# Loading the first row of a row-sum kernel by four strided loads of 32 partitions instead of one of 128

## Chip, cores, metric

One core of one Trainium2 chip. The metric is device time in microseconds (us) of one execution. The kernel before takes 162.29 us (median of 6 runs, 162.17 to 162.41).

## The reference

```python
def setup_inputs():
    batch, seq, dim = 32, 512, 1024
    return {"x": np.random.randn(batch, seq, dim).astype(np.float32)}

def reference(x):
    return np.sum(x, axis=-1).astype(np.float32)
```

16384 rows of 1024 floats are summed; 67.11 MB are read, next to nothing is written.

## The kernel before

The rows are laid over 128 partitions, 112 of them per partition in the first block and 16 in the second. VectorE sums tiles of 16 rows per partition; three tile buffers rotate. ScalarE helps at the very end only. Of the first tile, the first row of each partition has a load of its own. Two loads (`EARLY`) are moved ahead of the barrier with which the program opens.

```python
EARLY = 2
...
        while c < whole:
            m = min(G, whole - c)                       # G = 16 rows
            xt = xpool.tile([P, G * D], F32, tag="xt", name="xt")
            parts = (0, 1, m) if done + c == 0 else (0, m)
            for i, k in zip(parts, parts[1:]):
                nc.sync.dma_start(
                    out=xt[:, i * D : k * D], in_=x_b[:, (c + i) * D : (c + k) * D]
                )
            a = ACT_ROWS if done + c + m == full else 0
            rows_dve(xt, res, 0, m - a, c)
...
# after compiling: the first EARLY loads are taken out of the body and put before the opening barrier
    loads = [i for i in code if i.engine == sp][:EARLY]
...
    code[at:at] = loads
```

## Time and profile before

| | before |
|---|---|
| time | 162.29 us |
| span in the profile | 160.6 us |
| DMA engines occupied by the load queue | 97.2% |
| VectorE busy | 121.5 us (76%) |
| first reduce starts | 22.00 us |

The kernel is bound by its stream of loads: the 16 DMA engines go from one packet to the next without a gap, and everything else fits beside them. The prediction shows the lines for this.

### The profile page before, as it was taken

The page shows a single profiled execution, that of the slowest core. Times are in us where ns is not written, and L with a number is a line of the kernel's source. Part 1 is how long each engine was busy: PE and PEld are TensorE (multiplying, and loading weights), DVE is VectorE, ACT ScalarE, POOL GpSimd, SP SyncE. Part 2 cuts the span into 40 slices and gives each one's busy share as a digit, 9 for nine tenths or more (in the row PEclk, how much of TensorE's full clock was granted, in tenths as well). Part 3 has the DMA queues.
Part 4 walks back from the last instruction along what each step waited for, and adds up shares of the span by engine and source line. Part 5 has one row for each costly group of instructions (what it writes and reads, how often), then busy time and mean ns, then how long its engine had stood idle before and what let it go on. Part 6 is the DMA issues. An engine that isn't in the chain of part 4 may idle for free.

```text
span 160.6 us, 119 instructions
## 1 busy us (share of the span) xinstructions
DVE 121.5 (76%) x16; ACT 17.2 (11%) x31; POOL 0.2 (0%) x4
## 2 busy tenths in 40 slices
DVE  0000059997799959999499994999949998697884
ACT  0000000000000000000000000000000000695892
POOL 0000000000000000000000000000000000000000
DMA  9988996996996996996996996996996996998991
GB/s 375 490 367 367 490 522 277 506 522 277 506 522 261 522 522 261 522 522 261 522 506 277 522 506 277 522 506 277 522 506 277 522 490 294 441 431 364 436 390 44
DMA packets 2160, 67.18 MB, mean 418 GB/s; under 512 B 496, under 2 KB 624, under 8 KB 880
## 3 DMA queue, kind: packets, MB, share of 16 engines
q1 hardware_dynamic: 2016, 67.12, 97.2%
q10 hardware_dynamic: 144, 0.06, 0.1%
HBM read 67.11 MB, written 0.07 MB: 418 GB/s over the span
## 4 chain that ended last, share of the span: by engine, by line
DMA 75%; DVE 23%; SPq 0%; issue 0%; DVEq 0%
DMA xt<-in_x_dram 75%; DVE res L43 21%; DVE pairs L59 1%; SPq L95 0%; DVE seen L112 0%; DVE part L59 0%; DVE res L59 0%; DVEq L120 0%
## 5 line engine op out<-in xcount | busy, mean ns | idle before, releaser
L43 DVE TENSOR_REDUCE res<-xt 128x16 f32<-128x16384 f32 (+3 forms) x9 | 119.8, 13309 | 36.5 <-DMA xt<-in_x_dram 36.5
L51 ACT ACT_TABLE_LOAD x1 | 1.3, 1283 | 138.1 <-DMA xt<-in_x_dram 138.1
L51 ACT ACTIVATE xt<-xt 128x1024 f32<-128x1024 f32 x15 | 15.6, 1044 | 2.4 <-DMA xt<-in_x_dram 2.3
L51 ACT ACTIVATION_READ_ACCUMULATOR xt<-xt 128x1 f32 x15 | 2.8, 187 | 0.0
L59 DVE CUSTOM_DVE_ANT_0 pairs<-xt 128x512 f32<-128x512 f32 (+1 forms) x2 | 1.1, 567 | 0.2 <-DMA xt<-in_x_dram 0.2
L59 DVE CUSTOM_DVE_ANT_0 pairs<-xt,part 128x240 f32<-128x240 f32 x1 | 0.5, 468 | 0.0
L112 DVE COPY seen<-part 128x1 f32<-128x1 f32 x1 | 0.2, 153 | 0.0
L59 DVE DVE_READ_ACCUMULATOR2_ANT res<- 128x1 f32 x2 | 0.2, 83 | 0.0
L157 POOL MEMSET const-uint8-127<- 128x1 uint8 x1 | 0.1, 102 | 0.0
L157 POOL MEMSET const-bfloat16-1.0<- 128x1 bf16 x1 | 0.1, 101 | 0.0
L157 POOL MEMSET const-float32-0.0<- 128x1 f32 x1 | 0.1, 99 | 0.2 <-issue 0.2
L157 POOL MEMSET const-float32-1.0<- 128x1 f32 x1 | 0.1, 99 | 0.0
L59 DVE DVE_READ_ACCUMULATOR2_ANT part<- 128x1 f32 x1 | 0.1, 83 | 0.0
## 6 DMA issues: line engine op xcount, KB each, us to landing
xt<-in_x_dram SPq DMA_DIRECT2D x1, 7680.0 KB, 21.5
xt<-in_x_dram SPq DMA_DIRECT2D x1, 4608.0 KB, 32.5
xt<-in_x_dram SPq DMA_DIRECT2D x1, 2048.0 KB, 37.1
xt<-in_x_dram SPq DMA_DIRECT2D x1, 1024.0 KB, 39.1
xt<-in_x_dram SPq DMA_DIRECT2D x1, 512.0 KB, 3.8
xt<-in_x_dram SPq DMA_DIRECT2D x1, 272.0 KB, 39.3
xt<-in_x_dram SPq DMA_DIRECT2D x1, 240.0 KB, 39.4
xt<-in_x_dram SPq DMA_DIRECT2D x6, 40.8
```

Source lines behind the costliest of these rows:

```text
L43: nc.vector.tensor_reduce(out=res[:, c : c + n], in_=xt[:, j * D : (j + n) * D].rearrange("p (j d) -> p j d", d=D), axis=X, op=ADD,)
L51: nc.scalar.activation(out=v, in_=v, func=COPY, accum_out=acc)
L59: nc.vector.tensor_tensor_reduce(out=pairs[:, 0 : h - a], in0=xt[:, a:h], in1=xt[:, h:b], scale=1.0, scalar=first, op0=ADD, op1=ADD, accum ...
L112: nc.vector.tensor_copy(out=seen, in_=part)
L157: nc = _bacc.Bacc("TRN2", target_bir_lowering=False, num_devices=1)
```

## The change

The intent: shorter loads, of 128 KB in place of 512, were to get all engines going sooner, and every fourth partition was taken in place of blocks of 32.

```diff
-EARLY = 2
+EARLY = 5
...
-            parts = (0, 1, m) if done + c == 0 else (0, m)
-            for i, k in zip(parts, parts[1:]):
+            parts = [(slice(None), 0, m)]
+            if done + c == 0:
+                parts = [(slice(q, P, 4), 0, 1) for q in range(4)] + [(slice(None), 1, m)]
+            for q, i, k in parts:
                 nc.sync.dma_start(
-                    out=xt[:, i * D : k * D], in_=x_b[:, (c + i) * D : (c + k) * D]
+                    out=xt[q, i * D : k * D], in_=x_b[q, (c + i) * D : (c + k) * D]
                 )
```

## The prediction

What named a mechanism that no trace or run of this case shows is cut, and the cuts are marked: a paragraph of background, the reason given for a smaller spread, a reason for rival 1, and the mechanism of rival 2. The sum: 3.43 - 0.27 + 0.03 = 3.19 us, of whose gain of 0.24 I took 0.15, so 162.1. The 0.27 was my estimate, from the measured spread of 0.356 us taken in proportion to the rows of a load, 0.356 x 32 / 128 = 0.09; no run shows that the spread goes with the rows. The 0.03 is counted: in the profile the load queue has 16 packets of 4 bytes and 9 ns for each load, and its packets rose from 2016 to 2064 with three more loads. The 0.32 us of rival 2 is an estimate as well, twice the measured 0.159 us of a packet, and rival 3's reason is a supposition.

> **What bounds the kernel now.** I began with the page's busy shares and its DMA lines, to see which resource is full.
>
> ```profile
> DVE 121.5 (76%) x16; ACT 17.2 (11%) x31; POOL 0.2 (0%) x4
> ...
> DMA  9988996996996996996996996996996996998991
> ...
> q1 hardware_dynamic: 2016, 67.12, 97.2%
> ```
>
> VectorE is busy for 76% of the span, but the load queue occupies all 16 DMA engines for 97.2% of it. The sixes in the row of DMA tenths are no gaps: a 64 KB packet takes about 2.42 us and is counted in one slice, so slices of 4 us hold now one and now two of them per engine. Read from the records of single packets, each engine goes from one 64 KB packet to the next with nothing between. 8.39 MB (16 rows of 128 partitions) pass every 19.34 us, which is 434 GB/s.
>
> Next the chain of work that ended last, in order of time (start, length, what), to see whether VectorE ever holds the DMA back.
>
> ```profile
> 1.19 0.07 issue
> 1.26 39.99 DMA xt<-in_x_dram
> ...
> 41.27 17.23 DVE res L43
> ...
> 58.52 40.78 DMA xt<-in_x_dram
> ...
> 117.43 39.13 DMA xt<-in_x_dram
> 156.55 0.02 issue
> 156.58 0.69 DVE pairs L59
> ```
>
> The chain steps through VectorE because the load that it then follows was issued when a reduce freed its buffer. That must not be read as VectorE holding the end: the load issued at 58.52 landed 40.78 us later although its own packets need only 19.34. It stood in line for the other half. The packet records say the same: the load issued at 39.24 has its first packet at 59.50, so the line is never empty. A reduce takes 17.22 us and a load 19.34, so VectorE has 2.1 us to spare in every stage. The 1.7 us of VectorE at the end of the chain start when the last pieces land, and move with them.
>
> So the time is: when the DMA stream starts, plus a stream at a fixed rate, plus a fixed tail. The part that the change touches is the start. The same kernel by stretches of time (stretch, length, VectorE, ScalarE, GpSimd, clock, DMA share, GB/s):
>
> ```profile
> 0.00:1.00 1.00, 0.00 (x0) 0.00 (x0) 0.20 (x4) 1.00 0.00 0
> 1.00:2.00 1.00, 0.00 (x0) 0.00 (x0) 0.00 (x0) 1.00 0.94 164
> 2.00:3.00 1.00, 0.00 (x0) 0.00 (x0) 0.00 (x0) 1.00 2.12 897
> ```
>
> And the DMA issues, with the us from issue to landing:
>
> ```profile
> xt<-in_x_dram SPq DMA_DIRECT2D x1, 7680.0 KB, 21.5
> ...
> xt<-in_x_dram SPq DMA_DIRECT2D x1, 512.0 KB, 3.8
> ```
>
> Nothing moves in the first microsecond, and in the second 164 GB/s, well under half of 434, although the engines count as 94% busy: the packets are slow, not absent. (The 897 of the next line is the 60 KB packets credited as they start.) The records give the detail. The first load is issued from 0.000 to 0.376 and the second from 0.426 to 0.850. The first packets start on the 16 engines between 1.000 and 1.356. An engine carries eight 4 KB packets of the first row; most take 0.159 us, but 28 of the 128, mostly the first two of an engine, take 0.20 to 0.83, and the eight take 1.82 us on average (29.13 us over 16 engines) where 8 x 0.159 = 1.27 would do. The engines then start on the second load between 2.705 and 3.431, mean 3.00. This spread does not heal: before the last 64 KB packets, engines stand between 134.454 and 135.144, again 0.69 apart. A load has landed only when the slowest engine is through, so **the start of the slowest engine on the second load, 3.43 us, is what the change has to lower.**
>
> [...]
>
> **The change part by part.** It removes one issue of 512 KB and adds four of 128 KB (32 packets of 4 KB each). Bytes, packet size and number of packets stay the same; the three additional loads bring 3 x 16 semaphore packets, of 9 ns each, about 0.03 us per engine. All later loads keep their order. Five loads now stand before the opening barrier instead of two, and the other engines' waits on the first tile name five landings instead of two.
>
> Issue: the first load's 0.376 and a gap of 0.050 make 0.43 us per issue; the five loads at the end of the kernel, issued back to back at 116.569 to 118.412, are 0.46 apart. I assume that a load of 32 rows costs the same, as an issue seems mostly fixed. The second load then goes out at 4 x 0.43 = 1.7 us (1.84 at 0.46) instead of 0.43. From issue to first packet it took 1.000 in the first load and 0.845 in the final store (158.356 to 159.201), so its packets are ready on the first engine at 2.55 to 2.84, and 0.36 later on the last, if the spread of 1.000 to 1.356 is repeated: 2.9 to 3.2. That is close to the 2.705 to 3.431 at which the engines came to it before. The later issue costs nothing on the slow engines and holds the quick ones a little.
>
> Start:[...] The last engine then starts near 1.09, up to 0.27 earlier. The work after that is the same eight packets, the cold ones included, for they appear on every engine until about 2.0 us whatever its start. Each quarter brings an engine two packets, 0.32 us when warm, for 0.43 us of issue; but cold packets fill the difference for the first two quarters, so that only the quick engines run dry.
>
> Sum for the slowest engine: 3.43 - 0.27 (start) + 0.03 (semaphores) = 3.19, against a gate of 2.9 to 3.2 from the issue. I take half to two thirds of the 0.24 that this leaves, because the cold packets are a matter of chance, one unlucky engine sets the end, and the gate is so near: 0.15 us. 162.24 - 0.15 = 162.1.
>
> Beside other work, at no cost: the barrier opens near 2.5 us instead of 1.19, but VectorE first works at 22.0, and the next load, issued at 1.26 until now, is not reached in the line before 20.8. The three further waits of some 20 ns on VectorE and SyncE fall into its 2.1 us of slack.
>
> **The rivals.** (1) *The issue becomes the gate.* One issue of a load took 0.617 us (the fourth of the kernel). Were each quarter to cost that plus 0.05, the second load would go out at 2.67 and reach the last engine near 2.67 + 1.36 = 4.0: +0.6, so 162.8.[...] Against: 0.376 and 0.328 are the commoner values. (2)[...] a warm packet may take up to 0.32 us; six of them add 0.95 at worst, 163.2.[...] (3) *Cold packets shrink.* If they came from 128 rows being asked for at once, asking for 32 would make them quick: row done at 1.0 + 1.27 = 2.3 and, with the gate, the slowest engine near 2.9: -0.5, so 161.7. The gate forbids more. (4) *Hidden anyway*: cold packets last until 2.0 us whatever is done, and the time stays at 162.2.
>
> **Range and chances.** Rivals 1 and 2 pull up by up to 0.6 or 0.9, rival 3 down by 0.5; the three runs before span 0.2. Eight times in ten I expect 161.5 to 162.7. Two per cent are 3.24 us. The whole head up to the slowest engine's second load is 3.43 us, of which 1.00 + 1.27 cannot go; and a loss of that size would need the row to take more than twice as long. Within 2%: 98%.
>
> **What would show it.** In the stretches, 1.0 to 2.0 us should move somewhat more than 164 GB/s. The second load should be issued between 1.5 and 1.9 us, and land at 21.8 rather than at 21.9 (0.43 + 21.5). The first reduce should start near 21.85, not 22.00, and all later ones be shifted by the same amount; the reduces still 19.3 us apart. An issue of the second load after 2.2 us would be rival 1; 4 KB packets of 0.2 to 0.32 us still after 2.2 us, rival 2; hardly any over 0.2 us, rival 3. I am wrong in the principle if the start moves and the end doesn't follow it.

## The result and the profile after

| | before | after |
|---|---|---|
| time, median | 162.29 us (162.17 to 162.41, 6 runs) | 163.99 us (163.8 to 164.4, 6 runs) |
| ratio, 95% interval | | 1.0107 (1.0094 to 1.012) |
| span in the profile | 160.6 us | 162.2 us |
| fifteen-row load issued | 0.43 us | 2.49 us |
| first reduce starts | 22.00 us | 23.59 us |

A ratio is the mean time of one kernel's fast runs over the mean of the other's in the same rounds, so it isn't quite the ratio of the medians. The change costs 1.7 us, 1.1%: within 2%, but outside my range, and in the other direction from the small gain that I expected.

The SyncEngine's DMA issues in order of time (start, length). Before, one issue for the row and one for the fifteen rows:

```profile
0.00 0.85 SPq L81 DMA_DIRECT2D xt<-in_x_dram  x2
```

After, from two windows: the four quarters, then the fifteen rows:

```profile
0.00 2.45 SPq L83 DMA_DIRECT2D xt<-in_x_dram  x4
...
2.49 0.58 SPq L83 DMA_DIRECT2D xt<-in_x_dram  x1
```

A quarter costs 2.49 / 4 = 0.62 us of issue, not the 0.43 that a load of 128 rows cost. By itself it lasts 0.55 to 0.59 us (the first one, with nothing ahead of it, 0.547), where the row in one piece took 0.376.

The stretches of the changed kernel (stretch, length, VectorE, ScalarE, GpSimd, clock, DMA share, GB/s; packets are credited where they start, which makes shares above 1):

```profile
0.00:1.00 1.00, 0.00 (x0) 0.00 (x0) 0.20 (x4) 1.00 0.00 0
1.00:2.00 1.00, 0.00 (x0) 0.00 (x0) 0.00 (x0) 1.00 0.50 143
2.00:3.00 1.00, 0.00 (x0) 0.00 (x0) 0.00 (x0) 1.00 0.72 205
```

Before, the second microsecond had a share of 0.94 and the third was in full flow. Here the engines wait through both. Spreading each packet over its own duration gives the number of busy engines from the packet records:

| from, us | 1 | 2 | 3 | 4 | 5 |
|---|---|---|---|---|---|
| busy engines before | 12.9 | 16 | 16 | 16 | 16 |
| busy engines after | 6.9 | 11.6 | 10.9 | 13.0 | 16 |

The deficit is 18.5 engine-microseconds, or 1.16 us for each of the 16 engines. A second part hides inside packets that count as busy: an engine's first long packet of 60 KB took 2.267 us on every engine before and 2.27 to 3.07 after, mean 2.78, another 0.51. The eight short packets are 0.08 quicker on average (1.74 us in place of 1.82). Together 1.16 + 0.51 - 0.08 = 1.59, and the mean end of the first long packet did move from 5.26 to 6.91 us, by 1.65. On the slowest engine it moved from 5.70 to 7.28, by 1.58.

Nothing afterwards gives the time back or adds to it. The first reduces, before (start, length, waits):

```profile
22.00 17.22 DVE L43 TENSOR_REDUCE res<-xt 128x16 f32<-128x16384 f32 x1 [22.00 <-DMA xt<-in_x_dram]
41.27 17.22 DVE L43 TENSOR_REDUCE res<-xt 128x16 f32<-128x16384 f32 x1 [2.06 <-DMA xt<-in_x_dram]
```

and after:

```profile
23.59 17.22 DVE L43 TENSOR_REDUCE res<-xt 128x16 f32<-128x16384 f32 x1 [23.59 <-DMA xt<-in_x_dram]
42.84 17.22 DVE L43 TENSOR_REDUCE res<-xt 128x16 f32<-128x16384 f32 x1 [2.02 <-DMA xt<-in_x_dram]
```

The first is 1.59 later, the second 1.57, the span 1.6. The chain of waits ends in the same form as before, with the loads and then the same VectorE tail:

```profile
118.99 39.00 DMA xt<-in_x_dram
157.99 0.02 issue
158.01 0.69 DVE pairs L59
```

The last VectorE stretch begins at 158.01 in place of 156.58.

### The profile page after: what moved, and what is told of

It is laid out like the page before. It is cut to its first block, busy times and chain, and to the rows that moved or that the text cites. A ratio compares the mean times of both kernels' runs of the same rounds, so it can differ in the third digit from the quotient of the medians.

```text
span 162.2 us, 126 instructions
## 1 busy us (share of the span) xinstructions
DVE 121.5 (75%) x16; ACT 17.2 (11%) x31; POOL 0.2 (0%) x4
## 3 DMA queue, kind: packets, MB, share of 16 engines
q1 hardware_dynamic: 2064, 67.12, 96.5%
## 4 chain that ended last, share of the span: by engine, by line
DMA 73%; DVE 22%; SPq 0%; issue 0%; DVEq 0%
DMA xt<-in_x_dram 73%; DVE res L43 21%; DVE pairs L59 1%; SPq L97 0%; DVE seen L114 0%; DVE part L59 0%; DVEq L122 0%; DVE res L59 0%
```

## The experiments

My theory after the result, the **gate theory**: the fifteen-row load is issued so late that the engines run dry, and a long load that finds them dry starts slowly. Rivals: the four pieces themselves are slow in the DMA engines, or only the number of loads counts. Where an expectation named a mechanism that no run shows, those words are cut, and the cut is marked; the numbers expected stay. Eleven kernels ran, all with correct results. "First long packet" is an engine's first packet of the fifteen-row load (sixteen rows in one kernel), taken from the packet records; the last column of the table is when the slowest engine ended it in the profiled run.

| kernel | time, median (range), us | ratio | fifteen rows issued, us | slowest first long packet ended, us |
|---|---|---|---|---|
| before | 162.29 | | 0.43 | 5.70 |
| after | 163.99 (163.8-164.4) | 1.0107 | 2.49 | 7.28 |
| e1 quarter blocks | 163.48 (163.21-164.4) | 1.0082 | 1.80 | 6.58 |
| e2 columns | 165.2 (163.78-165.57) | 1.0162 | 1.84 | 6.84 |
| e3 quarters behind | 162.37 (162.32-162.47) | 1.0004 | 0 | 4.47 |
| e4 one load | 162.43 (162.41-162.45) | 1.0011 | 0 | 4.65 |
| e5 strided halves | 164.79 (164.57-164.9) | 1.0155 | 1.23 | 7.64 |
| e6 late issue | 164.18 (163.81-164.98) | 1.0126 | 1.83 | 8.26 |
| e8 half blocks | 165.03 (164.59-165.08) | 1.0165 | 1.23 | 8.47 |
| e9 behind the barrier | 162.63 (162.41-164.62) | 1.0056 | 0.78 | 6.14 |
| e10 two ahead | 163.24 (163.18-163.5) | 1.0062 | 1.22 | 6.16 |
| e11 halves, gap | 164.33 (163.56-165.2) | 1.0127 | 1.86 | 8.61 |

In e3, e4 and e10 some or all of the row does not lie ahead of that packet: 1.27 us (eight packets of 0.159) are to be added in e3, 0.64 in e10, and 1.06 in e4, whose seven further packets of 64 KB take 2.418 us each in place of 2.267. e7 is told by itself below.

### e3: the same pieces behind the long load

```diff
-parts = [(slice(q, P, 4), 0, 1) for q in range(4)] + [(slice(None), 1, m)]
+parts = [(slice(None), 1, m)] + [(slice(q, P, 4), 0, 1) for q in range(4)]
```

> The same five loads, but the fifteen-row load first and the four strided quarters behind it. Gate theory: the quarters' issues (still 0.55 to 0.59 us each) now lie beside a transfer of 18 us, so the whole loss goes: 162.0 to 162.4. Rival (the quarters take more time in the DMA engines[...]): the loss of 1.6 us stays, 163.9.

Measured: 162.37 us, ratio 1.0004 (0.9989 to 1.0019). The five issues, and the quarters' time to landing:

```profile
0.00 2.89 SPq L83 DMA_DIRECT2D xt<-in_x_dram  x5
```

```profile
xt<-in_x_dram SPq DMA_DIRECT2D x4, 128.0 KB, 20.1
```

The first reduce starts within 0.1 us of where it did before (22.00):

```profile
22.08 17.22 DVE L43 TENSOR_REDUCE res<-xt 128x16 f32<-128x16384 f32 x1 [22.08 <-DMA xt<-in_x_dram]
```

The issues are as dear as in the changed kernel (0.535 to 0.598 us each), but they lie beside the long load. All 128 short packets take 0.159 us, not one more. The whole loss is gone with no byte, packet or piece changed, only their order. So the strided pieces are not slow in themselves. In the changed kernel 49 of the 128 take over 0.2 us, but there the engines have nothing else in line, and even so the eight of an engine take no longer than before (1.74 us against 1.82).

### e10: two pieces ahead, two behind

```diff
+quarters = [(slice(q, P, 4), 0, 1) for q in range(4)]
+parts = quarters[:2] + [(slice(None), 1, m)] + quarters[2:]
```

> The same five loads as in the changed kernel, with two strided quarters ahead of the fifteen-row load and two behind it. Gate theory: the fifteen-row load is issued at 1.2 us, the slowest engine's first long packet ends at 5.7 to 6.1, and the two quarters behind it add 0.64: 6.3 to 6.8 where the kernel before has 5.70, so 162.9 to 163.4, between the 162.37 of none ahead and the 163.99 of four. Rival (only the last quarters, which find the engines empty, cost anything): 162.4 or 163.9.

Measured: 163.24 us, inside the range. With none, two and four quarters ahead the time is 162.37, 163.24 and 163.99: about 0.4 us for each. The fifteen rows went out at 1.22 and the slowest engine ended its first long packet at 6.16, 4.94 later. So the loss grows evenly, and isn't the work of the last pieces. The issue of the fifteen rows:

```profile
1.22 0.58 SPq L84 DMA_DIRECT2D xt<-in_x_dram  x1
```

One part of the theory does not fit. By the packet records, 13 of the 16 engines here begin their first long packet right behind a short one (within 10 ns), so they had not just run dry. Yet these 13 take 2.68 to 3.15 us, mean 2.94, as slow as on idle engines in e3 (2.92). Running dry is thus not needed for a slow first long packet. In e10 the packets started 1.3 to 1.7 us after the issue; in e9 below, where 1.8 to 2.2 us lay between, fifteen of 16 took 2.27 to 2.42. The late issue goes with the slow packet; by what mechanism is open.

### e1: blocks in place of strides

```diff
-(slice(q, P, 4), 0, 1)
+(slice(32 * q, 32 * q + 32), 0, 1)
```

> Four loads of 32 neighbouring partitions in place of every fourth one. Gate theory (the fifteen-row load is issued at 2.49 us in the changed kernel because an issue of 32 rows takes 0.55 to 0.59 us, and the engines run dry): if the step of four partitions makes the issue dear, the four issues fall to 0.33 to 0.43 us, the fifteen-row load goes out at 1.7 to 1.9 us and the time is about 163.2; if the small number of partitions makes it dear, the issues stay at 0.55 to 0.59, the load goes out at 2.5 and the time is 164.0 or more. Rival ([...]the issue is innocent): [...]the row takes longer still, 164.3 or more, whatever the issue takes.

Measured: 163.48 us. The four issues of e1, then the fifteen rows, from two windows:

```profile
0.00 1.76 SPq L83 DMA_DIRECT2D xt<-in_x_dram  x4
...
1.80 0.42 SPq L83 DMA_DIRECT2D xt<-in_x_dram  x1
```

Each issue takes 0.37 to 0.42 us, and the fifteen rows go out at 1.80, which is what my prediction had assumed for the change (1.70 to 1.84). The time is still 0.8% above before, and the slowest first long packet ends 0.88 us later than before (6.58 against 5.70). So dear issues are the smaller part of the loss: from e1 to the changed kernel the end of that packet moves by another 0.70. A caution: blocks have a cost of their own in the engines, which e7 shows (0.249 us a packet); here it lies in time in which the engines would partly be waiting (DMA share 0.79 from 1 to 2 us). But e2 and e6, without blocks and issued at 1.84 and 1.83, come out at 6.84 and, on fifteen of 16 engines, by 6.70.

### e2: the number of loads alone

```diff
-(slice(q, P, 4), 0, 1)
+(slice(None), q / 4, (q + 1) / 4)      # 128 partitions, 256 of the 1024 columns each
... (the addresses are made whole numbers)
```

> Four loads again, but each of all 128 partitions and a quarter of the row's columns (1 KB packets). If it is the number of loads alone, with 0.43 to 0.47 us for each, the fifteen-row load goes out at 1.75 to 1.9 us. In the changed kernel an issue later by 2.07 us moved the end by 1.6, so some 0.5 is hidden: 1.37 - 0.5 = 0.9 later than before, 163.2. Rival (loads of few partitions are slow in the DMA engines, and the issue is innocent): 162.3 to 162.5.

Measured: 163.78, 164.86, 165.54 and 165.57 us, ratio 1.0162 (1.0112 to 1.0211). The profiled run is the first and fastest of the four. It had issues of 0.375 to 0.432 us, the fifteen rows at 1.84 and the end of the slowest first long packet at 6.84, 5.00 after the issue. Loads of all partitions are no better, so few partitions per load are not needed for a loss. The loss is larger and more scattered than I expected; the other three runs have no trace, so what adds up to 1.8 us to them is open.

### e6: the row whole, only the issue late

```diff
+# between the row's load (128 partitions) and the fifteen rows, three times:
+nc.sync.dma_start(out=spare[:, 16 * s : 16 * s + 16], in_=x_b[:, 0:16])
```

> The kernel before with its row in one piece, but three small loads (64 bytes of each partition into a spare tile) between the row and the fifteen rows, so that the fifteen-row load is issued late with nothing else changed. With 0.45 us for each issue it goes out at 1.75 to 1.9 us. Gate theory: the slowest engine ends its first long packet 4.5 to 5.0 us after that issue, at 6.3 to 6.8 instead of 5.70, and the time is 162.9 to 163.4. Rival (the loss is due to the row's own pieces[...] and the late issue is hidden behind the row): 162.3 to 162.5.

Measured: 163.81 to 164.98 us, median 164.18; the profiled run is the slowest. The issues:

```profile
0.00 0.36 SPq L87 DMA_DIRECT2D xt<-in_x_dram  x1
0.41 1.37 SPq L86 DMA_DIRECT2D spare<-in_x_dram  x3
1.83 0.43 SPq L87 DMA_DIRECT2D xt<-in_x_dram  x1
```

With the row untouched and 24 KB added, a fifteen-row load issued at 1.83 costs 1.5 us or more. That is a late issue without any splitting, and the loss is above my range. The trace says why this run was so slow: fifteen engines ended their first long packet between 5.91 and 6.70, the last of them inside the 6.3 to 6.8 expected, and one engine started at 5.08 and ended at 8.26. One straggler sets the end of a load that all 16 share: the first reduce started at 24.54 us, in place of 22.00. It was held up in the small loads: their last packets ran from 4.65 to 5.08, when those of the other engines had ended by 3.81. So "nothing else changed" isn't quite so. The fifteen engines account for 6.70 - 5.70 = 1.0 us; the other three runs, which have no trace, lost 1.6 to 2.1, and the rest stays unexplained.

### e9: how much lateness is hidden

```diff
-EARLY = 2
+EARLY = 1        # in the kernel before
```

> The kernel before, but only the row's load is moved ahead of the opening barrier; the fifteen-row load is issued behind it, near 0.8 us instead of 0.43. Gate theory: 0.8 + 4.5 to 5.0 = 5.3 to 5.8 for the slowest engine's first long packet, against 5.70 set by the row ahead of it: the lateness is hidden or all but hidden, 162.2 to 162.5. Rival (every 0.1 us of later issue is 0.1 us at the end): 162.6 to 162.7.

Measured: 162.41, 162.55, 162.70 and 164.62 us; ratio 1.0056 with an interval from 0.9985 to 1.0126, so a difference isn't shown. One run lies in the theory's range, one between it and the rival's, one (162.70) in the rival's and the fourth in neither, so e9 doesn't decide between them. In the profiled run, 162.70, fifteen engines ended their first long packet by 5.21 and one at 6.14: it started at 3.00, no later than engines did before, but took 3.15 us. A later issue by 0.36 us is hidden on fifteen of the engines in this run, but stragglers appear already.

### e4: no row split off

```diff
-EARLY = 5
+EARLY = 1
-parts = [(slice(q, P, 4), 0, 1) for q in range(4)] + [(slice(None), 1, m)]
+parts = [(slice(None), 0, m)]
```

> The first tile as one load of sixteen rows, no row split off. In the kernel with the quarters last, which also starts with the long load, the slowest engine ended its first long packet 4.47 us after the first issue. If a load from idle engines needs these 4.5 us whatever it is (gate theory), the end is the same as before: 162.2 to 162.4. Rival (splitting off a row, as the kernel before does, has gained something by starting the engines on short packets): 162.7 or more.

Measured: 162.43 us, ratio 1.0011 (0.9995 to 1.0028). The first reduce starts where that of the kernel before does (22.00):

```profile
21.94 17.22 DVE L43 TENSOR_REDUCE res<-xt 128x16 f32<-128x16384 f32 x1 [21.94 <-DMA xt<-in_x_dram]
```

Splitting the row off gains nothing that these runs can tell. e3 and e4 also give the clean price of a start from idle engines, with nothing queued ahead. Their first packets start on the 16 engines between 0.99 and 1.71 us (e3) and between 1.00 and 1.88 (e4). The first long packet takes 2.92 us on average in e3, in place of 2.267 later in the same load. The slowest engine is through it 4.47 us after the issue began.

### e5, e8, e11: halves, which the theory does not cover

e5 has two loads of every second partition, e8 two blocks of 64, e11 is e5 with one small load ahead of the fifteen rows.

```diff
-(slice(q, P, 4), 0, 1) for q in range(4)
+(slice(q, P, 2), 0, 1) for q in range(2)              # e5, e11; EARLY = 3 and 4
+(slice(64 * q, 64 * q + 64), 0, 1) for q in range(2)  # e8; EARLY = 3
```

In e11's expectation the words for its first case are cut. That case was: the delay strikes only the load right behind the halves, so the small load suffers it in place of the fifteen rows.

> Two loads of every second partition, 64 each. If the step makes the issue dear, each takes 0.55 to 0.59 us, the fifteen-row load goes out at 1.25 us, 0.83 later than before; with 0.5 of it hidden the time is 162.6. If the number of partitions does, the issue should lie between 0.38 and 0.57, the load goes out near 1.0 and the time is 162.3 to 162.5. Rival[...]: between before and changed whatever the issue takes, near 163.1.

> Two blocks of 64 neighbouring partitions. The issue without a step takes 0.37 to 0.43 us, so the fifteen-row load goes out near 0.87 us. Gate theory: 0.87 + 4.5 to 5.0 = 5.4 to 5.9, about the 5.70 of before: 162.2 to 162.5. If pieces of 64 rows delay what follows for a reason other than their step (the strided halves were slower than their early issue explains), 164 or more.

> The two strided halves again, with one small load (64 bytes of each partition) between them and the fifteen rows. With the halves alone the fifteen-row load was issued at 1.23 us, but the engines took it up between 3.0 and 5.1 us, the last first long packet ended at 7.64, and the gate theory (1.23 + 4.5 to 5.0 = 5.7 to 6.2) does not hold. [...]the fifteen-row load, though issued at about 1.85, is over on the last engine at 6.4 to 7.0, and the time falls from 164.8 to 163.0 to 163.6. If the delay is from something else, the later issue adds to it: 164.8 or more.

All three missed: 164.79, 165.03 and 164.33 us, above the changed kernel although the fifteen rows went out earlier. The stretches of e5 show a hole that is not for want of an issue, which was over at 1.81 us:

```profile
1.00:2.00 1.00, 0.00 (x0) 0.00 (x0) 0.00 (x0) 1.00 0.65 98
2.00:3.00 1.00, 0.00 (x0) 0.00 (x0) 0.00 (x0) 1.00 0.95 385
3.00:4.00 1.00, 0.00 (x0) 0.00 (x0) 0.00 (x0) 1.00 1.24 471
```

By the packet records, 15.7 engines are busy from 2 to 3 us, then 7.5 and 10.2 in the next two: the row is over by 3.36, and the engines take up the fifteen rows one after another between 3.00 and 5.11. Blocks of 64 (e8) do the same, so the step of two is not the cause. My idea that only the next load is delayed fell with e11, where the small load took that place and the engines still came between 2.98 and 5.39. What delays the load behind pieces of 64 rows stays open. In e10 the fifteen rows went out at the same time as in e5 (1.22 and 1.23) and were through at 6.16 in place of 7.64, so here the issue time isn't what decides.

### e7: the shapes where the line is full

```diff
+# kernel before, with the first row of tiles 3 to 6 split: strided quarters, quarter blocks,
+# strided halves, half blocks
+rows = {2: [slice(q, P, 4) for q in range(4)], 3: [slice(32 * q, 32 * q + 32) for q in range(4)],
+        4: [slice(q, P, 2) for q in range(2)], 5: [slice(64 * q, 64 * q + 64) for q in range(2)]}
```

> The start as in the kernel before; the first rows of the third to sixth tiles are split in the four ways (strided quarters, quarter blocks, strided halves, half blocks), where some 20 us of transfers are always in line. Gate theory: nothing of it is seen in the time, 162.2 to 162.5. The issues by themselves: 0.53 to 0.60 us for pieces with a step, also where the issue before lies long back; 0.33 to 0.43 for blocks and whole loads. Rival (pieces cost time in the DMA engines wherever they stand): twelve pieces in place of four rows would cost over 1 us, 163.3 or more.

Measured, one run, state unknown: 165.11 us, a miss of the theory's number and in the range of its rival, but the trace parts the four shapes. Stretches around the four split rows, in the order above (the columns as before):

```profile
40.10:41.90 1.80, 0.84 (x1) 0.00 (x0) 0.00 (x0) 1.00 1.91 801
59.50:62.30 2.80, 1.27 (x1) 0.00 (x0) 0.00 (x0) 1.00 1.64 517
80.00:82.00 2.00, 0.62 (x1) 0.00 (x0) 0.00 (x0) 1.00 1.80 754
99.50:102.50 3.00, 1.32 (x1) 0.00 (x0) 0.00 (x0) 1.00 1.55 478
```

The two strided rows pass in 1.8 to 2.0 us, the two block rows need 2.8 to 3.0. (The long packets credited here put the rates above the true ones in all four alike.) By packet: strided quarters 0.159 us each without exception, strided halves 0.161 on average, quarter blocks 0.249, half blocks 0.264. On the slowest engine a block row takes 2.2 us in place of 1.27. So where the line is full, strided pieces are free and blocks cost about 1 us a row. The runs show the packet times, not the reason for them. My expectation had left a cost of blocks out. The two block rows account for about 1.9 of the 2.7 us by which the span of 163.3 exceeds that of before; the rest is small losses in the split tiles, among them 0.2 us in each of three fifteen-row loads.

The issues of quarter blocks, strided halves and half blocks, the first of each group, with no other issue close before it:

```profile
39.03 0.35 SPq L91 DMA_DIRECT2D xt<-in_x_dram  x1
...
58.31 0.48 SPq L91 DMA_DIRECT2D xt<-in_x_dram  x1
...
78.27 0.49 SPq L91 DMA_DIRECT2D xt<-in_x_dram  x1
```

A block of 32 is as cheap as a whole load (0.33), pieces of 64 are dear with and without a step; the strided quarters took 0.58 to 0.70. So my two simple rules of e1's expectation, that the step or the number of partitions makes an issue dear, are both wrong as they stand: 32 rows are cheap in a block and dear with a step of four, 64 rows are dear either way, 128 are mostly cheap. Shape isn't all: a load of 128 right behind dear pieces is dear too (the fifteen rows of the changed kernel, 0.58, shown above; 0.59 in e5 and e8), and the fourth load of the kernel before took 0.617 behind another whole one. Why is open.

## Why the prediction was wrong, point by point

- **What bounds the kernel** was right. The start moved by 1.59 us at the first reduce, and the end followed by 1.6 in the span. That the slowest engine on the second load decides it was right too (the last of its packets ended at 21.54 us before and 23.14 after, and the first reduce started at 22.00 and 23.59), but its start is not enough: the time that its first long packet takes counts as well. (The spread that it calls "again 0.69" was 0.73 at the start of that load.)
- **The cost of the issue** failed: "I assume that a load of 32 rows costs the same, as an issue seems mostly fixed." It cost 0.62 us with its gap, not 0.43, and the second load went out at 2.49, not 1.7. This was rival 1, which had it at 2.67 from the one long issue in the trace. By e1, whose issues were cheap, it makes 0.70 us of the later end, as far as the blocks' own cost is hidden there.
- **The gate** failed, and it is the larger part: "The later issue costs nothing on the slow engines and holds the quick ones a little." I had the engines start 1.00 to 1.36 us after the issue and take their long packets at the usual 2.27 us, thus the last one through 3.6 us after the issue. Measured, with the engines idle (e3): through after 4.47; in the changed kernel 4.79; with e1's issue, at the time I had assumed, 4.77 and a loss of 0.88 us. There are two errors in it. The 1.36 is not the start of the sixteenth engine: packet records carry no engine number, it is the nineteenth packet in order of start, some engines began their second packet by then, and e3 and e4 show the last engine at 1.71 and 1.88. And the first long packet of a late load takes up to 0.8 us more than in the stream (up to 3.07 in place of 2.267), on engines that had run dry and, in e10, on engines that had not. Before, both lay hidden behind the row's own packets; by this reading, that cover is what the later issue took away. Even rival 1, with nearly the right issue time, came out at 162.8 because it used the same gate.
- **The gain at the start** did not come: 0.27 us earlier on the last engine was expected, but the first packet itself came at 1.317 in place of 1.000. The issue was longer by 0.17 of that (0.547 against 0.376). A stretch of 1 to 2 us with more than 164 GB/s was to show the gain; it had 143.
- **Slow packets** were said to come until 2.0 us whatever is done. Before, 26 of the 28 had started by then, the last at 2.23. After, 49 packets of 128 took over 0.2 us, and they came up to 3.5 us, after each time that an engine had stood empty; in e3, behind a full line, none did. They go with an engine's start from empty more than with the time since the kernel began.
- **Packets of up to 0.32 us** (rival 2) are out for strided pieces in a full line: 0.159 to 0.161 us per packet in e3 and e7. The sign that was to show it, packets of 0.2 us and more still after 2.2 us, came all the same, so it was a poor sign. Blocks do have slower packets in e7 (0.249 and 0.264); why is not shown.
- **Beside other work**: the barrier, which SyncEngine passed at 3.4 us in place of 1.2, and the further waits cost nothing visible, as said; e3 has them and is as fast as before.

What was not shown: why some issues are dear, why the packets of blocks are slower, why the first long packet of a late load is slow, what holds the load behind pieces of 64 rows, and which engine becomes a straggler. None of the versions tried beats the kernel before; e3 and e4 equal it.

## What to carry to other kernels

What to look at is how long the next big load needs from issue to flow and how much work the queue holds until then. At the start of this stream of loads it was 4.47 us to the end of the first 60 KB packet on the slowest of 16 engines (e3; 4.65 in e4); the small loads put ahead of the big one pushed its issue out by 0.4 to 0.6 us each and brought it little cover (0.32 us for a quarter of this row at 0.159 us a packet). The gate is not the whole story: pieces of 64 partitions cost more than it allows, 2.5 us in all (e5) and 2.8 (e8). Small loads in a full line were free here when they were strided (e3, 162.37 us against 162.29), and cost about 1 us a row in blocks (e7). An issue on SyncEngine took 0.33 to 0.47 us for 128 partitions in the kernel before, except one of 0.62; 0.35 to 0.42 for blocks of 32 (e1, and the first in e7); 0.48 to 0.61 for 64 partitions (e7); and 0.53 to 0.70 for 32 with a step of four (after, e3, e7). When reading packets from a trace, don't take one of the first packets for one engine each, and look for start-up costs inside "busy" packets as well as between them.
